# Three spaced groups of seven products in each FFN's down product, and x kept in two of five shared buffers

## The chip, the cores and the metric

The kernel runs on one core of one Trainium2 chip. The metric is the device time of one execution in microseconds. Three executions of the kernel before took 1870.79, 1872.24 and 1873.25 us; their median, 1872.24 us, is the time before. The core works with a tensor engine (PE, with its weight loads shown apart as PEld), a vector engine (DVE), a scalar engine (ACT), GpSimd (POOL), and a sync engine (SP) that issues most of the transfers.

## The reference

One layer of a streaming encoder on 256 rows of width 2048, all in float32:

```
x += 1/2 * (silu(n1 @ w_gate) * (n1 @ w_up)) @ w_down      n1 = RMSNorm(x)      (FFN 1)
u | q | k | v = RMSNorm(x) @ w_in
x += concat(RMSNorm(S5(u)), RMSNorm(attention(q, k, v))) @ w_out
x += 1/2 * (silu(n2 @ w_gate) * (n2 @ w_up)) @ w_down      n2 = RMSNorm(x)      (FFN 2)
x += RMSNorm((p @ w_ple_proj) * sigmoid(RMSNorm(x) @ w_ple_gate))
```

The hidden width of the FFNs is 5632. The two products `@ w_down` (256 x 5632 by 5632 x 2048) are what the change is about; w_gate and w_up are 2048 x 5632 each.

## The kernel before

**Precision.** Every float32 operand of a matmul is split into a rounded part and a rest (`split`, L165 to L173): a cast on ACT writes `hi` (L168), a subtraction on DVE writes `lo` (L171). A product is then three matmuls: hi by hi, lo by hi, hi by lo.

**Tiles.** The 256 rows are two row tiles `t` of 128. Weights come in raw tiles of 128 x 4 x 512 (four blocks of 128 along the contraction, one column block of 512; 1 MB, one transfer on SP, L282). A raw tile is split in two halves of 128 x 1024, `whi` and `wlo`, in four buffers each. A half feeds 12 matmuls of 128x128 by 128x512: two blocks, two row tiles, three matmuls (`gemm_half`, L285). Raw tiles have three buffers. So PE can be at most about four halves behind DVE, and the transfers at most three raw tiles ahead of the splits.

**FFN.** The hidden values are written as `hT` (transposed blocks of 32 that SP's small transfers set in order, L216). `act(k)` (L586) splits four of the 44 contraction blocks into `hhi` and `hlo`, in two buffers. The down product before goes through the four column blocks of 512 one after the other (L591): eleven raw tiles each, `act(k)` made anew for each of them, the sum of a column block in two banks of PSUM (tag `acc`, four of them), then two instructions that add half of it to the residual x (L594), then the next norm's work for this block (`nxt.block`, L357: DVE transposes, sixteen small transfers on SP, four scaled splits, squares on ACT).

**Groups of seven.** In FFN 2 the first four contraction blocks of gate and up are already done together, by seven products of sums in place of eight (`gemm_seven`, L428, Winograd's form of Strassen's scheme). The left-hand sums are made once (`sum_forms`, L409); the right-hand sums are four DVE additions of weight halves (L459), whose splits go to `shi` and `slo`, three buffers each. The order is products 1, 2, 5, 6, 4, 7, 3. The other twelve contraction blocks follow as plain columns. FFN 1 has no such groups.

**Order.** The program hands the instructions over in an order, and a planner orders them per engine from that. `step()` (L100) is called after each half and moves side work (`put_off`) on by one.

**x.** The residual x is in eight tiles of its own (pool `xres`, L53 and L140) from start to end. It is read for the squares of the first norm, changed by the down product of FFN 1, by w_out, by the down product of FFN 2, and by the last line.

Of the kernel before, what the change touches and what calls it, by code (L numbers as in the profile page):

```python
# [33 lines left out]
def layer_kernel(ctx: ExitStack, tc: tile.TileContext, a: dict, shapes: dict, out: bass.AP):  # L34
# [18 lines left out]
    xpool = ctx.enter_context(tc.tile_pool(name="xres", bufs=1))  # L53
# [10 lines left out]
    def uid(s):  # L64
        count[0] += 1
        return f"{s}_{count[0]}"
# [161 lines left out]
    def in_32(u):  # L228
        return u.rearrange("p j (x b) -> p j x b", b=32)
# [7 lines left out]
    def first_quarters(w, xn):  # L237

        rest = com("h")
        raws = [wp.tile([P, 4, NB], F32, tag="raw", name=uid("raw"), bufs=3) for _ in range(2)]  # L240
# [36 lines left out]

    def weight_halves(w, k0, nk, n0, own=None):

        raw = wp.tile([P, 4, NB], F32, tag="raw", name=uid("raw"), bufs=3)  # L280
        src = w[k0 * P : (k0 + nk) * P, n0 : n0 + NB].rearrange("(j p) n -> p j n", p=P)
        nc.sync.dma_start(raw[:, :nk, :], src)  # L282
        return weight_split(raw, nk, own)
# [122 lines left out]
        def rs(self, t):  # L406
            return self.r[:, t : t + 1]

    def sum_forms(parts):  # L409

        hi, lo = parts
        whole, sums = com("h"), com("h")
        u = whole.rearrange("p (j t m) -> p j t m", j=4, t=TT)
        nc.vector.tensor_tensor(
            out=whole.rearrange("p (j t) -> p j t", j=4), in0=hi.bitcast(F32), in1=lo.bitcast(F32), op=ALU.add
        )
        s = sums.rearrange("p (z j m) -> p z j m", z=4, j=2)
        up, down = u[:, :2], u[:, 2:]
        for z, (x, y, op) in enumerate((
            (up[:, :, 1], down[:, :, 1], ALU.subtract), (s[:, 0], up[:, :, 0], ALU.subtract),  # L420
            (up[:, :, 0], up[:, :, 1], ALU.subtract), (down[:, :, 0], s[:, 1], ALU.add),
        )):
            nc.vector.tensor_tensor(out=s[:, z], in0=x, in1=y, op=op)
        both = halves("n")
        split(*both, sums.rearrange("p (z t) -> p z t", z=4))
        return both

    def gemm_seven(act, sums, ws, n0, nkt, pool, first, second):  # L428

        raws = []  # L430
        for w in ws:
            raw = wp.tile([P, 4, NB], F32, tag="raw", name=uid("raw"), bufs=3)
            nc.sync.dma_start(raw, w[: 4 * P, n0 : n0 + NB].rearrange("(j p) n -> p j n", p=P))
            raws.append(raw)
        b11, b21, b12, b22 = (raw[:, 2 * h : 2 * h + 2, :] for raw in raws for h in range(2))
        parts = act(0)

        def whole(k, t):
            return [[u[:, 2 * k + j, t * P : (t + 1) * P] for j in range(2)] for u in parts]

        def summed(z):
            return [[u[:, z, j * P : (j + 1) * P] for j in range(2)] for u in sums]

        def product(ps, left, src, own, stop):
            hi, lo = (
                (pool if own else wp).tile([P, 2, NB], F32R, tag=s, name=uid(s), bufs=3 if own else None)
                for s in (("shi", "slo") if own else ("whi", "wlo"))
            )
            split(hi, lo, src)
            lh, ll = left  # L450
            for j in range(2):
                nc.tensor.matmul(ps, lhsT=lh[j], rhs=hi[:, j], start=j == 0, stop=False)  # L452
                nc.tensor.matmul(ps, lhsT=ll[j], rhs=hi[:, j], start=False, stop=False)  # L453
            for j in range(2):
                nc.tensor.matmul(ps, lhsT=lh[j], rhs=lo[:, j], start=False, stop=stop and j == 1)  # L455

        def add(x, y):
            t = pool.tile([P, 2, NB], F32, tag="sum", name=uid("sum"), bufs=2)
            nc.vector.tensor_tensor(out=t, in0=x, in1=y, op=ALU.add)  # L459
            return t  # L460

        p1, p2 = acc(), acc()
        product(p1, whole(0, 0), b11, False, True)
        product(p2, whole(1, 0), b21, False, False)
        step()
        t1 = add(b11, b12)
        p5 = acc()
        product(p5, summed(0), t1, True, True)
        t2 = add(t1, b22)
        p67 = aux()  # L470
        product(p67[:, :NB], summed(1), t2, True, True)
        step()
        t4 = add(t2, b21)
        p4 = acc()
        product(p4, whole(1, 1), t4, True, False)
        t3 = add(b12, b22)
        product(p67[:, NB:], summed(2), t3, True, True)
        step()
        p38 = aux()
        product(p38[:, :NB], summed(3), b22, False, False)  # L480
        step()
        put_off(0, first, p1, p67)
        for w, banks, fresh in ((ws[0], [p2, p4], False), (ws[1], [p38[:, :NB], p38[:, NB:]], True)):
            for k0 in range(4, nkt, 4):
                part = act(k0 // 4)
                for half in list(weight_halves(w, k0, 4, n0)):
                    begin = k0 == 4 and half[0] == 0
                    end = k0 + 4 >= nkt and half[0] == 1
                    for t in range(TT):
                        gemm_half({t: banks[t]}, (part, half), (t,), fresh and t == 1 and begin, end)  # L490
                    step()
            if not fresh:
                put_off(0, second, p2, p4, p5)
        return p38

    def ffn(i, xn, nxt, bg=None):
        wg, wu, wd = (a[f"ffn{i}_w_{s}"][0] for s in ("gate", "up", "down"))
# [22 lines left out]
        for f in range(NF):  # L520
# [5 lines left out]
            if sevens and f:  # L526
                sg, hh = com("sg"), com("h")
                gate_cols, up_cols = ([u[:, t * NB : (t + 1) * NB] for t in range(TT)] for u in (sg, hh))

                def opened(p1, p67, g=gate_cols, u=up_cols):  # L530
                    nc.scalar.copy(g[0], p1)
                    nc.vector.tensor_tensor(out=u[0], in0=p67[:, :NB], in1=g[0], op=ALU.add)
                    nc.vector.tensor_tensor(out=u[1], in0=p67[:, NB:], in1=u[0], op=ALU.add)

                def gated(p2, p4, p5, g=gate_cols, u=up_cols, hh=hh):
                    for z, (ps, other) in enumerate(((p2, g[0]), (p4, u[1]))):
# [3 lines left out]
                    nc.vector.tensor_tensor(  # L540
                        out=v, in0=p5.unsqueeze(1).to_broadcast([P, TT, NB]), in1=v, op=ALU.subtract
                    )

                p38 = gemm_seven(xn, sums, (wg, wu), f * NB, KD, sevens, opened, gated)
                nc.vector.tensor_tensor(out=hh, in0=p38, in1=hh, op=ALU.add)
# [15 lines left out]
            if f == 0 and not bg:  # L561
                both = gemm_pair(xn, ((wg, 0), (wu, 0)), KD)
                pg = next(both)
                sums = sum_forms(xn(0))
            else:
                pg = gemm_block(xn, wg, f * NB, KD, first)
            sg = com("sg")
# [15 lines left out]
                )  # L583
            put_off(2, turned, hp, f, hh)

        def act(k):  # L586
            hi, lo = halves("h")
            split(in_32(hi), in_32(lo), hT[k // 2][:, k % 2 * 4 : k % 2 * 4 + 4])
            return hi, lo

        for n in range(ND):  # L591
            ps = gemm_block(act, wd, n * NB, F // P)
            for t in range(TT):
                nc.vector.scalar_tensor_tensor(  # L594
                    out=xt[t][n], in0=ps[t], scalar=0.5, in1=xt[t][n], op0=ALU.mult, op1=ALU.add
                )
            put_off(0 if n == ND - 1 and n < nxt.early else 2, nxt.block, n)
        pools.close()


# [734 lines left out]
    for n, side in ((0, 0), (1, 0), (0, 1), (1, 1), (2, 0), (2, 1), (3, 0), (3, 1)):  # L1335
        y, r = ((yss, rss), (ysb, rsb))[side]
        ps = next(both) if n < 2 and not side else gemm_block(lambda k: y[k], sides[side], n * NB, SW // P)
        for t in range(TT):
            nc.vector.scalar_tensor_tensor(
                out=xt[t][n], in0=ps[t], scalar=r[0][:, t : t + 1], in1=xt[t][n], op0=ALU.mult, op1=ALU.add  # L1340
            )
        if side:
            put_off(0 if n == ND - 1 else 2, n2.block, n)
    atp.close()
    mix.close()
# [205 lines left out]
```

## Time and profile before

| | |
|---|---|
| median of three executions | 1872.24 us |
| the profiled execution | 1872.24 us |
| its span, first to last instruction | 1870.4 us |
| granted clock of the tensor engine | 1.000 |
| matmuls, busy share of PE | 9134, 99% |
| busy share of PEld, DVE, ACT, POOL | 82%, 70%, 53%, 3% |
| share of 16 DMA engines, transfers issued by SP | 63.7% |
| down product of FFN 1 | about 491 to 730 us |
| gate and up of FFN 2 with groups of seven | about 1097 to 1523 us |
| down product of FFN 2 | about 1523 to 1763 us |

The span is what lies between the first and the last instruction. A matmul record is longer than the distance to the next one, since matmuls are pipelined; what counts is the distance from start to start. In the lists, "idle before" is the time an engine stood still before an instruction, with what ended it. Idle time of ACT or DVE costs nothing as long as PE is fed.

### The profile page before, as it was taken

The numbers are of one execution on the slowest core, as the hardware profiler recorded it, in microseconds if no ns is written. First come the engines' busy times: TensorE is split into PE (matmuls) and PEld (weight loads), VectorE is DVE, ScalarE is ACT, GpSimd is POOL, SyncE is SP. The second block draws the span as 40 slices with busy tenths as digits, with TensorE's granted clock in tenths as the row PEclk, the third lists the DMA queues.
The fourth block names the chain that finished last, engine by engine and source line by source line (L and its number), as shares of the span: only waits on it lengthen the run. The fifth ranks groups of instructions, "written<-read, shape, count | busy, mean of one in ns | idle before, by whom it ended". The sixth has DMA issues, their size and how long they took to land.

```text
span 1870.4 us, 23938 instructions
## 1 busy us (share of the span) xinstructions
PE 1859.4 (99%) x9134; PEld 1536.3 (82%) x9134; DVE 1310.4 (70%) x1527; ACT 996.5 (53%) x1151; POOL 50.4 (3%) x84
## 2 busy tenths in 40 slices
PE   9999999999999999999999999999999999999998
PEld 7888888888888888878888888888888888888887
DVE  8867665455576776687567678778787866777655
ACT  7444444444456665456695555445454555666554
POOL 0011000000000000010020000000000000000000
PEclk9999999999999999999999999999999999999999
DMA  8788867766655666675645666575666675656563
GB/s 323 242 278 268 267 208 222 231 217 200 217 196 199 212 199 244 185 248 163 222 147 189 218 205 221 203 220 186 203 205 208 225 228 203 204 202 212 189 224 124
DMA packets 230387, 400.06 MB, mean 214 GB/s; under 512 B 26401, under 2 KB 50337, under 8 KB 229985
## 3 DMA queue, kind: packets, MB, share of 16 engines
q1 hardware_dynamic: 227824, 392.81, 63.7%
q0 software_dynamic: 1728, 4.33, 0.7%
q8 instruction: 71, 1.16, 0.3%
q10 hardware_dynamic: 720, 1.41, 0.2%
q14 instruction: 44, 0.35, 0.1%
HBM read 369.26 MB, written 9.83 MB: 203 GB/s over the span
## 4 chain that ended last, share of the span: by engine, by line
PE 92%; ACT 3%; DVE 2%; DMA 1%; SPq 1%; issue 1%; POOL 0%; DVEq 0%; ACTq 0%; POOLq 0%
PE acc L292 26%; PE acc L297 26%; PE acc L293 26%; PE aux L293 3%; PE aux L292 3%; PE aux L297 3%; ACT whi L168 1%; SPq L1061 1%; PE acc L455 1%; DMA raw<-in_w_in 1%; PE aux L452 1%; PE acc L452 1%; PE acc L453 1%; PE aux L455 1%; PE aux L453 1%
## 5 line engine op out<-in xcount | busy, mean ns | idle before, releaser
L171 DVE TENSOR_TENSOR wlo<-raw,whi 128x1024 fp32r<-128x1024 f32 x656 | 798.2, 1224 | 458.9 <-ACT whi L168 455.3
L168 ACT CAST whi<-raw 128x1024 fp32r<-128x1024 f32 x656 | 686.2, 1053 | 758.7 <-PE acc L293 607.9
L292 PE MATMUL acc<-whi,nhi 128*128 128x512 f32 x1408 | 551.0, 391 | 1.2 <-ACT whi L260 0.5
L293 PE MATMUL acc<-whi,nlo 128*128 128x512 f32 x1408 | 548.2, 389 | 0.0
L297 PE MATMUL acc<-wlo,nhi 128*128 128x512 f32 x1408 | 384.4, 389 | 0.0
L292 PE MATMUL acc<-whi,hhi 128*128 128x512 f32 x816 | 317.6, 389 | 0.0
L293 PE MATMUL acc<-whi,hlo 128*128 128x512 f32 x816 | 317.5, 389 | 0.0
L292 PEld LDWEIGHTS acc<-whi,nhi 128*128 128x128 f32 x1408 | 264.3, 188 | 58.3 <-ACT whi L168 1.7
L297 PEld LDWEIGHTS acc<-wlo,nhi 128*128 128x128 f32 x1408 | 264.2, 188 | 55.6 <-DVE wlo L171 0.4
L293 PEld LDWEIGHTS acc<-whi,nlo 128*128 128x128 f32 x1408 | 264.4, 188 | 54.0
L297 PE MATMUL acc<-wlo,hhi 128*128 128x512 f32 x816 | 221.0, 389 | 0.0
L297 PEld LDWEIGHTS acc<-wlo,hhi 128*128 128x128 f32 x816 | 152.8, 188 | 32.5 <-DVE wlo L171 0.9
L293 PEld LDWEIGHTS acc<-whi,hlo 128*128 128x128 f32 x816 | 153.2, 188 | 32.0
L292 PEld LDWEIGHTS acc<-whi,hhi 128*128 128x128 f32 x816 | 153.1, 188 | 31.8
L171 DVE TENSOR_TENSOR hlo<-hT,hhi 128x1024 fp32r<-128x1024 f32 x88 | 107.1, 1218 | 0.0
L168 ACT CAST hhi<-hT 128x1024 fp32r<-128x1024 f32 x88 | 91.8, 1044 | 0.5 <-PE acc L455 0.4
L292 PE MATMUL aux<-whi,nhi 128*128 128x512 f32 x160 | 62.2, 389 | 0.0
L293 PE MATMUL aux<-whi,nlo 128*128 128x512 f32 x160 | 62.2, 389 | 0.0
L297 PE MATMUL aux<-wlo,nhi 128*128 128x512 f32 x160 | 49.3, 389 | 0.0
L171 DVE TENSOR_TENSOR slo<-sum,shi 128x1024 fp32r<-128x1024 f32 x40 | 48.6, 1214 | 0.4 <-ACT shi L168 0.2
L168 ACT CAST shi<-sum 128x1024 fp32r<-128x1024 f32 x40 | 42.1, 1052 | 11.5 <-DVE sum L459 11.4
L297 PEld LDWEIGHTS aux<-wlo,nhi 128*128 128x128 f32 x160 | 30.0, 188 | 6.2
(312 smaller groups left out, 1314.5 us busy)
## 6 DMA issues: line engine op xcount, KB each, us to landing
raw<-in_ffn_w_up SPq DMA_DIRECT2D x88, 1024.0 KB, 5.9
raw<-in_ffn_w_down SPq DMA_DIRECT2D x88, 1024.0 KB, 5.0
raw<-in_ffn_w_gate SPq DMA_DIRECT2D x86, 1024.0 KB, 5.4
raw<-in_w_in SPq DMA_DIRECT2D x32, 1024.0 KB, 5.5
raw<-in_w_out SPq DMA_DIRECT2D x16, 1024.0 KB, 5.1
raw<-in_w_ple_gate SPq DMA_DIRECT2D x16, 1024.0 KB, 5.1
hT<-mid SPq DMA_DIRECT2D x160, 64.0 KB, 5.0
h<-mid SPq DMA_DIRECT2D x176, 32.0 KB, 3.4
```

The lines of the kernel that those rows point to most:

```text
L168: copy = nc.scalar.copy(hi, src)
L171: nc.vector.tensor_tensor(out=lo, in0=src, in1=hi.bitcast(F32), op=ALU.subtract)
L292: nc.tensor.matmul(ps[t], lhsT=lh, rhs=hi[:, j, cols], start=start and j == 0, stop=False)
L293: nc.tensor.matmul(ps[t], lhsT=ll, rhs=hi[:, j, cols], start=False, stop=False)
L297: nc.tensor.matmul(ps[t], lhsT=lh, rhs=lo[:, j, cols], start=False, stop=stop and j == 1)
L452: nc.tensor.matmul(ps, lhsT=lh[j], rhs=hi[:, j], start=j == 0, stop=False)
L453: nc.tensor.matmul(ps, lhsT=ll[j], rhs=hi[:, j], start=False, stop=False)
L455: nc.tensor.matmul(ps, lhsT=lh[j], rhs=lo[:, j], start=False, stop=stop and j == 1)
L1061: nc.sync.dma_start(zt[0][p1 : p1 + HC, z], sv[p0 : p0 + HC, r % 2 * 2 + r // 2])
```

## The change

Four things change.

1. The pool of x goes. x lies in two raw buffers (`place_x`), and raw tiles get five buffers. The buffers of x are given back between its uses: x is read again at the start of the down product of FFN 1 from the input, and at that of FFN 2 from a scratch tensor `scr_x`, which w_out's end writes. These transfers (8 of 256 KB for each, `fetch_x`, and 8 for the write) are issued on POOL.
2. The down product handles two column blocks at once, with all eight PSUM banks. A plain step `c` multiplies four contraction blocks into both column blocks, and splits `act` once for both (`kept`). A step `s` does the same four by a group of seven. `a5` does the rest, side by side. The first pair has two groups, the second one.
3. Since the left-hand sums differ from group to group, `sum_forms` runs for each, from `hT`; the results of the products that both columns share are added to x as soon as the last group of a pair is through (`opened`).
4. `gemm_seven` becomes a class, used in FFN 2's gate and up too, with its products in the order 1, 5, 6, 4, 7, 2, 3. A pool `sums1` is opened for FFN 1's down product.

```diff
-    xt = [[xpool.tile([P, NB], F32, name=f"x_{t}_{n}") for n in range(ND)] for t in range(TT)]
+    def place_x():
+        for t in range(TT):
+            x = wp.tile([P, ND, NB], F32, tag="raw", name=uid("x"), bufs=5)
+            xt[t][:] = [x[:, n, :] for n in range(ND)]
+
+    def fetch_x(rows):
+        place_x()
+        for n in range(ND):
+            for t in range(TT):
+                nc.gpsimd.dma_start(xt[t][n], rows[t * P : (t + 1) * P, n * NB : (n + 1) * NB])
...
-        raw = wp.tile([P, 4, NB], F32, tag="raw", name=uid("raw"), bufs=3)
+        raw = wp.tile([P, 4, NB], F32, tag="raw", name=uid("raw"), bufs=5)
...
+        def chunk(self, kb, final=()):
+            raws = []
+            for w, n0 in self.ws:
+                raw = wp.tile([P, 4, NB], F32, tag="raw", name=uid("raw"), bufs=5)
...
+                raws.append(raw)
+            b11, b21, b12, b22 = (raw[:, 2 * h : 2 * h + 2, :] for raw in raws for h in range(2))
+            parts, sums = self.act(kb), self.sums(kb)
...
+            self.product(1, whole(0, 0), b11, False, final)
+            t1 = self.add(b11, b12)
+            self.product(5, summed(0), t1, True, final)
+            step()
+            t2 = self.add(t1, b22)
+            self.product(6, summed(1), t2, True, final)
+            t4 = self.add(t2, b21)
+            self.product(4, whole(1, 1), t4, True, final)
+            step()
+            t3 = self.add(b12, b22)
+            self.product(7, summed(2), t3, True, final)
+            self.product(2, whole(1, 0), b21, False, final)
+            step()
+            self.product(3, summed(3), b22, False, final)
+            step()
+
+        def column(self, side, kbs, final=False):
+            zs = ((2, 4), (3, 8))[side]
+            w, n0 = self.ws[side]
+            for kb in kbs:
+                part = self.act(kb)
+                for half in list(weight_halves(w, 4 * kb, 4, n0)):
+                    end = final and kb == kbs[-1] and half[0] == 1
+                    for t in range(TT):
+                        ps = self.bank(zs[t])
+                        gemm_half({t: ps}, (part, half), (t,), self.begin(zs[t]), end)
+                    step()
...
-        for n in range(ND):
-            ps = gemm_block(act, wd, n * NB, F // P)
-            for t in range(TT):
-                nc.vector.scalar_tensor_tensor(
-                    out=xt[t][n], in0=ps[t], scalar=0.5, in1=xt[t][n], op0=ALU.mult, op1=ALU.add
-                )
-            put_off(0 if n == ND - 1 and n < nxt.early else 2, nxt.block, n)
+        def opened(s, n):
+            sg = com("sg")
+            one, six = sg[:, :NB], sg[:, NB:]
+            nc.scalar.copy(one, s.bank(1))
+            nc.vector.tensor_tensor(out=six, in0=s.bank(6), in1=one, op=ALU.add)
+            gather(xt[0][n], one, 0.5)
+            for t in range(TT):
+                gather(xt[t][n + 1], s.bank(5), 0.5)
+            gather(xt[0][n + 1], six, -0.5)
+            nc.vector.tensor_tensor(out=one, in0=s.bank(7), in1=six, op=ALU.add)
+            gather(xt[1][n], one, 0.5)
+            gather(xt[1][n + 1], one, -0.5)
+
+        plans = (
+            ("c2", "c3", "s0", "c4", "c5", "c6", "s1", "c7", "c8", "c9", "c10"),
+            ("c1", "c2", "s0", "c3", "c4", "a5"),
+        )
+        for n in range(0, ND, 2):
...
+            for u in plan:
+                kb, final = int(u[1:]), u == plan[-1]
+                if u[0] == "s":
+                    left -= 1
+                    s.chunk(kb, () if left else shared)
+                    if not left:
+                        put_off(0, opened, s, n)
+                    continue
+                for side in range(2):
+                    s.column(side, (kb,) if u[0] == "c" else range(kb, F // P // 4), final)
+                    if final:
+                        end(side)
```

Here `end(side)` adds a column block's two own banks to x (two instructions as at L594) and puts off `nxt.block` for it, and `gather` is the instruction of L594 with a scale.

More of the change, by code (lines that the diff above doesn't have):

```diff
@@ L239, in first_quarters @@
         rest = com("h")
[L240 removed]
+        raws = [wp.tile([P, 4, NB], F32, tag="raw", name=uid("raw"), bufs=5) for _ in range(2)]
         src = [w[i * NB : (i + 1) * NB, :NB].rearrange("(j p) n -> p j n", p=P) for i in range(2)]
@@ L457, in add @@
-        def add(x, y):
-            t = pool.tile([P, 2, NB], F32, tag="sum", name=uid("sum"), bufs=2)
+                nc.tensor.matmul(ps, lhsT=lh[j], rhs=lo[:, j], start=False, stop=z in final and j == 1)
+        def add(self, x, y):
+            t = self.pool.tile([P, 2, NB], F32, tag="sum", name=uid("sum"), bufs=2)
             nc.vector.tensor_tensor(out=t, in0=x, in1=y, op=ALU.add)
             return t
-        p1, p2 = acc(), acc()
-        product(p1, whole(0, 0), b11, False, True)
-        product(p2, whole(1, 0), b21, False, False)
@@ L491, in gemm_seven @@
                     step()
-            if not fresh:
-                put_off(0, second, p2, p4, p5)
-        return p38
+    shared = (1, 5, 6, 7)
     def ffn(i, xn, nxt, bg=None):
```

146 lines of the change are left out of this document (84 added, 62 removed).

## The prediction

> **What bounds the kernel now.** I read the page's busy times first, then the waits, then the stages one by one.
>
> ```profile
> span 1870.4 us, 23938 instructions
> PE 1859.4 (99%) x9134; PEld 1536.3 (82%) x9134; DVE 1310.4 (70%) x1527; ACT 996.5 (53%) x1151; POOL 50.4 (3%) x84
> ```
>
> PE is busy for 99% of the span, so all other engines have room on the average. The waits say who follows whom:
>
> ```profile
> ACT whi L168 <- PE acc L293: 607.9, 432, 3.0
> DVE wlo L171 <- ACT whi L168: 455.3, 385, 7.4
> ACT whi L168 <- DMA raw<-in_ffn_w_gate: 22.2, 10, 5.1
> ```
>
> ACT's cast of a weight half stood still 432 times until PE had let go of a `whi` buffer. So the splits run as far ahead of PE as four buffers allow, and wait there. The stage of FFN 2's down product, and PE's chain at its start:
>
> ```profile
> 1523.40:1763.00 239.60, 239.60 (x1059) 198.40 (x1058) 170.63 (x160) 142.41 (x156) 0.00 (x0) 1.00 0.61 208
> ```
> ```profile
> 1523.45 0.23 PE acc L292
> ...
> 1526.17 0.23 PE acc L292
> ```
>
> The columns of the first are the stretch, its length, then the busy time of PE, PEld, DVE, ACT and POOL, the granted clock 1.00, the share of the DMA engines and GB/s. PE never stops. From one half's first matmul to the next half's it is 2.72 us for 12 matmuls: 0.2267 us each. The stage has 4 column blocks x 22 halves x 12 = 1056 matmuls, 239.4 us at this rate, and took 239.6. So a matmul taken out here is worth 0.2267 us, as long as PE stays fed.
>
> **The matmuls removed.** A plain step on two column blocks has 4 halves x 12 = 48 matmuls, a group of seven 7 x 6 = 42. There are three groups in each FFN's down product, six in all: 36 matmuls, 36 x 0.2267 = 8.2 us less.
>
> The page's PEld row, 1536.3 us in 9134 loads, is 0.168 us each, well under 0.2267. The Trainium skill (Perfetto Trace Analysis, Identifying the Most-Contended Engine) holds matmul busy time to be a poor measure of headroom, and points to the share of weight loads instead, here 82%. If only that were worth something, the 36 would give 6.1 us rather than 8.2. The stage's own length, 0.2267 us per matmul with no pause, speaks against that, and the sum goes by it.
>
> **What a group asks of DVE.** The prices, from groups and timelines:
>
> ```profile
> 1181.33 1.23 DVE L171 TENSOR_TENSOR slo<-sum,shi 128x1024 fp32r<-128x1024 f32 x1
> 1182.47 1.22 DVE L171 TENSOR_TENSOR wlo<-raw,whi 128x1024 fp32r<-128x1024 f32 x1
> 1183.61 1.22 DVE L545 TENSOR_TENSOR h<-aux,h 128x1024 f32<-128x1024 f32 x1
> ```
> ```profile
> L423 DVE TENSOR_TENSOR h<-h,h 128x256 f32<-128x256 f32 x2 | 0.8, 422 | 0.0
> L594 DVE SCALAR_TENSOR_TENSOR x<-acc,x 128x512 f32<-128x512 f32 x16 | 10.3, 686 | 8.7 <-PE acc L297 8.7
> L180 DVE SCALAR_TENSOR_TENSOR nlo<-h,gains,nhi 128x256 fp32r<-128x256 f32 x52 | 22.8, 489 | 1.2 <-ACT nhi L178 1.2
> ```
>
> DVE starts its 1024-wide instructions 1.14 us apart. A plain step needs four `wlo` and one `hlo`, 5.7 us of DVE in 48 x 0.2267 = 10.9 us of PE. A group needs `hlo`, four left-hand sums of 0.42, `nlo`, seven `lo` splits and four additions: 13 x 1.14 + 1.7 = 16.5 us of DVE in 42 x 0.2267 = 9.5 us of PE. It draws 7.0 us on the lead. How large is the lead?
>
> ```profile
> 1514.92 1.05 ACT L168 CAST whi<-raw 128x1024 fp32r<-128x1024 f32 x1 [0.71 <-ACT hhi L168]
> 1516.01 1.23 DVE L171 TENSOR_TENSOR wlo<-raw,whi 128x1024 fp32r<-128x1024 f32 x1 [0.35 <-ACT whi L168]
> 1523.29 0.39 PE L292 MATMUL acc<-whi,hhi 128*128 128x512 f32 x1
> ```
>
> These are one half's cast, its split, and PE's first matmul on it. DVE is through at 1517.15, 6.1 us before PE begins that half, and 8.9 us before PE begins the next one. So call T the start of PE on a group: DVE begins on it at T - 8.9. In the program's order it ends `hlo` at -7.8, the sums at -6.1, `nlo` at -4.9, then product 1 at -3.8, 5 at -1.5, 6 at 0.8, 4 at 3.1, 7 at 5.3, 2 at 6.5, 3 at 7.6. PE takes 1.36 us per product and wants the `lo` part 0.9 us after a product begins: at 0.9, 2.3, 3.6, 5.0, 6.3, 7.7 and 9.1. The tightest is product 7 with 1.0 us to spare. A group that starts with a full lead is covered. Between the two groups of the first pair lie three plain steps, which give back 3 x (10.9 - 5.7) = 15.6 us, more than the 7.0 drawn. ACT has nine casts at the 1.05 us shown, 9.5 us, in the same time, and is no bound.
>
> **What stands behind the last group of a pair.** There `opened` adds the shared products to x, eight DVE instructions of 0.61 us (L594's pairs, 1.3 us for two), 4.9 us, after an ACT copy. Queued behind it on DVE are the splits of the second column. After the group: `hlo` 8.7, two `wlo` 9.9 and 11.0, `opened` 15.9, the next `wlo` 17.1, wanted at 9.5 + 5.4 + 0.9 = 15.9: up to 1.2 us late. In the second pair the norm's scaled splits for two column blocks come due in the same step, since both blocks of the first pair ended together: L180 four times each, 1.7 us for one block ahead of that split, so up to 2.9 us late. Worst case over both FFNs: 2 x 1.2 + 2 x 2.9 = 8.2 us; best case 0, and no gain below it, since PE can't run faster than fed. In between, the groups in gate and up show how PE behaves when DVE is this late:
>
> ```profile
> 1148.86 0.93 PE aux L455 x4
> ...
> 1489.84 0.97 PE aux L455 x4
> ```
>
> Between these lie eight of the ten blocks with a group, 42.62 us each. Each has 42 + 144 = 186 matmuls, 42.16 us. Only 0.46 us per block is lost, although DVE is busy without pause there. PE's order has other matmuls between. I take 0.2 us for a first group, 0.6 for the one with `opened`, and 1.0 for the one with `opened` and the norms: 1.8 per FFN, 3.6 us.
>
> The saved `act` splits (44 before, 28 after per FFN) and the rest of the added DVE work lie beside PE and cost nothing: DVE was busy 170.6 of 239.6 us. If DVE filled up, that cover would be gone at once.
>
> **Gate and up of FFN 2.** The ten groups lose 10 x 0.46 = 4.6 us now. The new order splits products 1 and 5 first. The old one put two `wlo` ahead of the first addition:
>
> ```profile
> 1177.66 1.23 DVE L171 TENSOR_TENSOR wlo<-raw,whi 128x1024 fp32r<-128x1024 f32 x1 [1.45 <-ACT whi L168]
> 1178.80 1.22 DVE L459 TENSOR_TENSOR sum<-raw,raw 128x1024 f32<-128x1024 f32 x1
> ```
>
> This `wlo` waited for a `whi` buffer and the addition stood behind it. In the new order the addition has one such wait fewer in front, 2.72 us, and five raw buffers bring its weights sooner. Product 7, the last with an addition, is wanted at the same place but product 2 is then later by one split, so up to 0.23 us per group could be lost instead: bounds -4.6 and +2.3. I take half the loss, -2.3 us.
>
> **x and the transfers.** What was the cost of load and store of x elsewhere:
>
> ```profile
> raw<-in_ffn_w_down SPq DMA_DIRECT2D x88, 1024.0 KB, 5.0
> h<-mid SPq DMA_DIRECT2D x176, 32.0 KB, 3.4
> x<-in_x SPq DMA_DIRECT2D x8, 256.0 KB, 8.6
> coef<-scr_coef POOLq DMA_DIRECT2D x32, 64.0 KB, 6.6
> L788 POOL DMA_DIRECT2D coef<-scr_coef x32 | 15.4, 489 | 64.3 <-DVE t L841 57.4 <-DMA scr_coef<-cft 4.8 <-DMA coef<-scr_coef 1.2
> ```
>
> POOL gets 24 transfers of 256 KB more, at some 0.5 us of issue each 12 us on an engine that is 3% busy. Nothing waits for x until `opened`, some 70 us into the first pair. Its 2 MB delay weight tiles a little; the lead of a tile covers it. Bounds 0 and, if one tile per FFN came late by the 3.6 us between 5.0 and 8.6, 7.2 us; I take 0. SP gets two norm blocks' small transfers at once, 32 of them in the second pair at the pace of this row:
>
> ```profile
> 1587.91 2.51 SPq L216 DMA_DIRECT2D h<-mid  x4
> ```
>
> 0.63 us each, 20 us, spread over plain steps and the group, with raw tiles issued between: nothing, since the norm's splits come 13 halves later.
>
> **The sum.** -8.2 (matmuls) + 3.6 (late DVE) - 2.3 (gate and up) = -6.9 us. The profiled execution took 1872.24 us with 1870.4 us of span, and is itself the median. 1872.2 - 6.9 = 1865.3 us.
>
> **Rivals.**
>
> All is covered. PE fills each gap with ready matmuls, the loss in gate and up goes too: 1872.2 - 8.2 - 4.6 = 1859.4 us. For it: the table above has room at each product. Against it: the same room did not quite do in gate and up.
>
> DVE behind the groups gives the gain back: the worst case of 8.2 us, gate and up unchanged, 1872.2 us, no difference. For it: the planner keeps to program order on DVE, as L459 behind `wlo` shows, and `opened` is eight instructions in a row.
>
> The raw buffers bind (slower). During a down product x holds two of five, three are left, and a group holds two until its last split. In the new order product 2's split is the last reader of the first tile, up to T + 6.5, instead of the fourth addition. The tile that follows is issued then, lands after L, is cast in 1.05 us, and is wanted at T + 9.5 + 5.4 = 14.9: it is late when L exceeds 14.9 - 6.5 - 0.4 - 1.05 = 7.0 us. The median is 5.0, but all raw tiles spread widely:
>
> ```profile
> DMA to landing us min/median/max: 3.2/5.4/10.8
> ```
>
> With two tiles issued together and 9 us each, six groups lose 2 us, 12 us beyond my sum: 1877.3 us; at 10.8 us, 3.8 x 6 = 22.8, 1888 us. Against it: gate and up had three buffers, and the waits there (22.2 us on ACT) hardly reached PE.
>
> **Chances.** The forecast 0.50, all covered 0.14, gain given back 0.20, raw buffers 0.16. Two runs of this kernel can be told apart at about 0.2%, 3.7 us. The forecast and the first rival are faster, the second is within, the third slower; a little of the forecast's spread falls within 3.7 us, which I set off against the second's: faster 0.63, same 0.21, slower 0.16. The range goes from all covered to the raw buffers at 9 us: 1859.4 to 1877.3 us.
>
> **What would show it.** In the profile after: 36 matmuls fewer; FFN 2's down product about 235.4 + 1.8 = 237.2 us long in place of 239.6; blocks of gate and up with a group at 42.4 us in place of 42.62; in the second pair, behind the group, PE waiting for DVE's `wlo`. Wrong it is if ACT's casts there wait for raw tiles and PE with them (third rival), if a group has PE idle by more than 2 us, or if x's tiles keep weight tiles from being issued at the start of a down product.

## The result, and the profile after

| | before | after |
|---|---|---|
| median of four executions each | 1872.32 us | 1860.15 us |
| lowest and highest | 1870.79, 1873.25 us | 1859.97, 1860.21 us |
| the profiled execution, and its span | 1872.24, 1870.4 us | 1859.97, 1858.1 us |

The ratio is 0.9934, with a 95% interval of 0.9921 to 0.9947: faster by 0.66%, some 12 us. The page after, and two lines of its waits (engine, what it waited for, total us, times, longest):

```profile
span 1858.1 us, 23916 instructions
...
PE 1848.8 (100%) x9098; PEld 1530.4 (82%) x9098; DVE 1350.9 (73%) x1599; ACT 991.8 (53%) x1147; POOL 62.8 (3%) x108
```
```profile
ACT whi L181 <- PE acc L306: 497.9, 336, 3.0
DVE wlo L184 <- ACT whi L181: 398.7, 319, 7.3
```

There are 36 matmuls fewer, 9134 to 9098. DVE's share rose from 70% to 73%, and ACT and DVE still mostly wait for PE to let go of weight buffers.

Where did the 12.3 us between the two profiled executions go? The same five places in both traces mark the stages: the last hidden block of FFN 1; the four matmuls that stand ahead of the norm's eight transposes behind FFN 1's down product; the one plain hidden block of FFN 2; its last hidden block with a group; and the first result of the last line. Before, four rows of the timeline (start, length, engine, line, operation) and one of the chain:

```profile
490.41 1.41 DVE L580 SCALAR_TENSOR_TENSOR h<-acc,sm,sg 128x512 f32<-128x512 f32 x2 [1.09 <-PE acc L297]
...
1098.72 1.40 DVE L580 SCALAR_TENSOR_TENSOR h<-acc,sm,sg 128x512 f32<-128x512 f32 x2
...
1523.49 1.23 DVE L545 TENSOR_TENSOR h<-aux,h 128x1024 f32<-128x1024 f32 x1 [0.86 <-PE aux L297]
...
1802.39 1.27 ACT L1375 ACTIVATE h<-acc,sm 128x512 f32<-128x512 f32 x2
```
```profile
737.21 0.91 PE acc L297 x4
```

and after:

```profile
490.49 1.41 DVE L628 SCALAR_TENSOR_TENSOR h<-acc,sm,sg 128x512 f32<-128x512 f32 x2 [1.09 <-PE acc L310]
...
1092.92 1.40 DVE L628 SCALAR_TENSOR_TENSOR h<-acc,sm,sg 128x512 f32<-128x512 f32 x2
...
1514.93 1.23 DVE L593 TENSOR_TENSOR h<-aux,h 128x1024 f32<-128x1024 f32 x1 [0.86 <-PE aux L310]
...
1790.11 1.27 ACT L1476 ACTIVATE h<-acc,sm 128x512 f32<-128x512 f32 x2
```
```profile
733.57 0.91 PE acc L310 x4
```

| stage | before | after | difference |
|---|---|---|---|
| down product of FFN 1 | 246.80 | 243.08 | -3.7 |
| the middle: w_in, S5, attention, w_out, the first block of gate and up | 361.51 | 359.35 | -2.2 |
| gate and up of FFN 2 with groups | 424.77 | 422.01 | -2.8 |
| down product of FFN 2 | 278.90 | 275.18 | -3.7 |
| start and end of the span | | | +0.1 |

The two pairs of FFN 2's down product, then gate and up of FFN 2 from the first block with a group to the last, as stretches with busy times (columns as in the prediction):

```profile
1514.90:1632.10 117.20, 117.20 (x517) 96.85 (x517) 95.23 (x95) 63.45 (x64) 0.00 (x0) 1.00 0.59 200
1632.10:1750.60 118.50, 118.50 (x524) 97.99 (x523) 92.95 (x96) 73.33 (x89) 0.00 (x0) 1.00 0.66 219
```
```profile
1134.40:1514.90 380.50, 380.50 (x1675) 314.19 (x1675) 304.73 (x297) 194.05 (x199) 4.36 (x8) 1.00 0.67 214
```

PE never stops in any of them, as it did not before in the down product. The first pair has 528 - 12 = 516 matmuls, 117.0 us at 0.2267 us, and took 117.2. (Lengths of pairs below are taken from the last hidden block's row, and from the rows that add a pair's last column block to x.) The rest lies in the groups themselves. This is the first matmul of FFN 1's second group, and the first one behind the group:

```profile
554.55 0.39 PE L480 MATMUL acc<-whi,hhi 128*128 128x512 f32 x1
...
564.19 0.39 PE L305 MATMUL acc<-whi,hhi 128*128 128x512 f32 x1
```

The 42 matmuls between took 9.64 us without a pause, 229.5 ns each in place of 226.7: 0.12 us more for the group. All 16 groups of this trace, in the down products and in gate and up, have this distance; no run shows why it is longer. In gate and up, before, PE stood still for a little:

```profile
1140.10:1523.50 383.40, 382.83 (x1675) 312.73 (x1674) 304.67 (x296) 191.54 (x199) 0.00 (x0) 1.00 0.66 213
```

The nine blocks between the first and the last end took 383.3 / 9 = 42.59 us each before, and 380.5 / 9 = 42.28 after, where 186 matmuls at 0.2267 us make 42.16; the 0.12 left after is the group's longer distance. The waits of this stage show what went. Before, weight tiles came late, and PE then waited for splits:

```profile
ACT whi L168 <- DMA raw<-in_ffn_w_gate: 15.2, 8, 2.4
...
PEld aux L452 <- ACT shi L168: 2.7, 5, 0.6
```

After, the same view of the same stage has no line of a raw tile and none in which PE or its weight loads wait.

### The profile page after: what moved, and what is told of

Same layout as the page of the kernel before. It is cut to its first block, busy times and chain, and to the rows that moved or that the text cites. A ratio compares the mean times of both kernels' runs of the same rounds, so it can differ in the third digit from the quotient of the medians.

```text
span 1858.1 us, 23916 instructions
## 1 busy us (share of the span) xinstructions
PE 1848.8 (100%) x9098; PEld 1530.4 (82%) x9098; DVE 1350.9 (73%) x1599; ACT 991.8 (53%) x1147; POOL 62.8 (3%) x108
## 4 chain that ended last, share of the span: by engine, by line
PE 96%; ACT 2%; DVE 1%; DMA 0%; POOL 0%; issue 0%; SPq 0%; DVEq 0%; POOLq 0%
PE acc L305 22%; PE acc L310 22%; PE acc L306 22%; PE aux L306 7%; PE aux L305 7%; PE aux L310 7%; PE acc L480 2%; PE acc L481 2%; PE acc L483 2%; PE aux L480 1%; PE aux L481 1%; PE aux L483 1%; PE aux L1114 0%; ACT whi L181 0%; DMA raw<-in_ffn_w_gate 0%; ACT nhi L191 0%
## 5 line engine op out<-in xcount | busy, mean ns | idle before, releaser
L305 PE MATMUL acc<-whi,hhi 128*128 128x512 f32 x416 | 161.8, 389 | 0.0
L306 PE MATMUL acc<-whi,hlo 128*128 128x512 f32 x416 | 161.8, 389 | 0.0
L305 PE MATMUL aux<-whi,hhi 128*128 128x512 f32 x384 | 149.4, 389 | 0.0
L306 PE MATMUL aux<-whi,hlo 128*128 128x512 f32 x384 | 149.4, 389 | 0.0
L310 PE MATMUL acc<-wlo,hhi 128*128 128x512 f32 x416 | 126.7, 389 | 0.0
L310 PE MATMUL aux<-wlo,hhi 128*128 128x512 f32 x384 | 118.2, 389 | 0.0
L306 PEld LDWEIGHTS acc<-whi,hlo 128*128 128x128 f32 x416 | 78.1, 188 | 16.2
L305 PEld LDWEIGHTS acc<-whi,hhi 128*128 128x128 f32 x416 | 78.1, 188 | 16.2
L310 PEld LDWEIGHTS acc<-wlo,hhi 128*128 128x128 f32 x416 | 78.1, 188 | 16.2
L310 PEld LDWEIGHTS aux<-wlo,hhi 128*128 128x128 f32 x384 | 72.1, 188 | 15.0
```

What stands on the lines that cost most here:

```text
L305: nc.tensor.matmul(ps[t], lhsT=lh, rhs=hi[:, j, cols], start=start and j == 0, stop=False)
L306: nc.tensor.matmul(ps[t], lhsT=ll, rhs=hi[:, j, cols], start=False, stop=False)
L310: nc.tensor.matmul(ps[t], lhsT=lh, rhs=lo[:, j, cols], start=False, stop=stop and j == 1)
```

## The experiments

All times are medians in us; the kernel before, run beside them on the same chips, took 1871.57 (first four), 1871.36 (next four) and 1870.85 (last three). The kernel after has only its first four executions, beside which the kernel before took 1872.32: differences to 1860.15 carry this shift of up to 1.5 us, and the stage lengths from the traces are the surer ones.

**No groups.** How much of the gain is the removed matmuls, and does x in the raw buffers cost anything by itself? Every step of the down products is plain:

```diff
-            ("c2", "c3", "s0", "c4", "c5", "c6", "s1", "c7", "c8", "c9", "c10"),
-            ("c1", "c2", "s0", "c3", "c4", "a5"),
+            ('c0', 'c1', 'c2', 'c3', 'c4', 'c5', 'c6', 'c7', 'c8', 'c9', 'c10'),
+            ('c0', 'c1', 'c2', 'c3', 'c4', 'a5'),
```

> The changed kernel with every group of seven in the two down products made a plain step: the pairs of column blocks, x in two of five buffers and the new order in gate and up stay. It has as many matmuls as the kernel before. If the groups bring what the two traces say (36 matmuls of 0.2267 us less about 0.7 us of stalls), it takes 1860.15 + 7.4 = 1867.6 us. If part of the gain comes from handling two column blocks at once (fewer splits), it is well under that: 1864 us. If gate and up's gain needs nothing of the groups, their ten blocks stay at 42.28 us each.

It took 1867.73 (ratio to before 0.9980, 0.9972 to 0.9989). The groups are worth 1867.73 - 1860.15 = 7.6 us, of 36 x 0.2267 = 8.2. The 0.6 us that are missing are those of the groups' longer distance, 6 x 0.12 = 0.7: their DVE work costs PE nothing that shows. The other 3.8 us of the gain are there without them, 2.8 of them in gate and up, whose nine blocks take 42.28 us like those after. Two column blocks at once and x fetched on POOL thus cost nothing that shows.

**The old order in gate and up.** The prediction put the gain there down to the order 1, 5, 6, 4, 7, 2, 3. Here gate and up alone go back to the old one, with five raw buffers:

```diff
+            if early_two:
+                self.product(1, whole(0, 0), b11, False, final)
+                self.product(2, whole(1, 0), b21, False, final)
+                step()
+                t1 = self.add(b11, b12)
+                self.product(5, summed(0), t1, True, final)
...
-                s.chunk(0, shared)
+                s.chunk(0, shared, True)
```

> The changed kernel, with gate and up's groups in the order of before (products 1, 2, 5, 6, 4, 7, 3); the down products keep the new order. Theory order: the 0.32 us per block that gate and up gained comes from the first addition standing behind one cast fewer; then 1863.1 us, blocks of 42.6 us. Theory buffers: it comes from five raw buffers; then 1860.15 us, blocks of 42.28 us.

**x stays.** The buffers of x are never given back, so that three are left for weights everywhere, as before; the order is the new one:

```diff
-        fetch_x(a["x"][0] if bg else scr_x)
...
-            for t in range(TT):
-                nc.gpsimd.dma_start(scr_x[t * P : (t + 1) * P, n * NB : (n + 1) * NB], xt[t][n])
```

> The changed kernel, with x put into its two raw buffers once and left there: no second and third reading, no scratch tensor, and three raw buffers for weights everywhere, as before. Theory order: 1860.15 us, blocks of gate and up 42.28 us. Theory buffers: 1863.1 us, blocks of 42.6 us. If reading x again costs anything, it is gone here as well and the time falls below 1860 us.

**The kernel before with the new order** (and its three raw buffers):

```diff
-        p1, p2 = acc(), acc()
+        p1 = acc()
         product(p1, whole(0, 0), b11, False, True)
-        product(p2, whole(1, 0), b21, False, False)
-        step()
         t1 = add(b11, b12)
...
         product(p67[:, NB:], summed(2), t3, True, True)
+        p2 = acc()
+        product(p2, whole(1, 0), b21, False, False)
         step()
```

> The kernel before, with only the order of the products in gate and up's groups changed to 1, 5, 6, 4, 7, 2, 3. Theory order: 1872.3 - 3.0 = 1869.3 us. Theory buffers: 1872.3 us. Its instructions up to 1097 us are those of before, so the pause of 1.45 us in the tensor engine at 821 us, which the changed kernel doesn't have, should be there if it hangs on where the instructions lie.

The three give, with the kernels before and after, a table of block times in gate and up (span of the nine blocks, by nine) beside the medians:

| | order 1, 2, 5, 6, 4, 7, 3 | order 1, 5, 6, 4, 7, 2, 3 |
|---|---|---|
| three raw buffers | 42.59 (before) | 43.56 (before with new order, 1878.91, ratio 1.0037, 1.0025 to 1.0050) |
| three left beside x | | 43.21 (x stays, 1871.71, ratio 0.9999, 0.9990 to 1.0008) |
| five raw buffers | 42.28 (old order, 1860.03, ratio 0.9940, 0.9928 to 0.9953) | 42.28 (after, 1860.15) |

The order does nothing with five buffers, and with three the new one costs 0.6 to 1.0 us a block. No expectation had foreseen this: they put the kernel before with the new order at 1869.3 or 1872.3 us, and x staying at 1860.2 or 1863.1. The buffers make the gain, and keep the new order from costing what it costs with three, 7.3 us by the medians (1878.91 - 1871.57). Why, the place of a block's first addition `t1` shows, against the end of the block before it (the row `h<-aux,h`). Before, then after, then with x staying:

```profile
1178.80 1.22 DVE L459 TENSOR_TENSOR sum<-raw,raw 128x1024 f32<-128x1024 f32 x1
1183.61 1.22 DVE L545 TENSOR_TENSOR h<-aux,h 128x1024 f32<-128x1024 f32 x1
```
```profile
1164.91 1.22 DVE L487 TENSOR_TENSOR sum<-raw,raw 128x1024 f32<-128x1024 f32 x1
...
1177.53 1.22 DVE L593 TENSOR_TENSOR h<-aux,h 128x1024 f32<-128x1024 f32 x1
```
```profile
1172.73 1.22 DVE L486 TENSOR_TENSOR sum<-raw,raw 128x1024 f32<-128x1024 f32 x1
...
1176.58 1.22 DVE L592 TENSOR_TENSOR h<-aux,h 128x1024 f32<-128x1024 f32 x1
```

With five buffers the group's DVE work begins 12.6 us before the other block ends, with three 4.8 us (old order) or 3.9 us (new order). An addition reads both raw tiles of its group: both must be there while the tiles of the columns before are still held. With x staying, ACT waits in this stage for the tiles once more:

```profile
ACT whi L180 <- DMA raw<-in_ffn_w_gate: 29.4, 13, 2.9
```

The executions with x staying lay from 1868.14 to 1873.42; the profiled one is the lowest, 8.2 us above that after, and its nine blocks account for (43.21 - 42.28) x 9 = 8.4 us of it. In four of them PE stands still for 1.5 us, until ACT has split a sum. The kernel before with the new order has the same four pauses, and right behind two of them, at 1361.4 and at 1450.1 us, the granted clock (before the DMA share in the row) was halved for 3.4 us:

```profile
1360.98 0.50 PE L452 MATMUL acc<-shi,hhi 128*128 128x512 f32 x1 [1.47 <-ACT shi L168]
```
```profile
1361.40:1364.80 3.40, 3.40 (x10) 2.63 (x9) 3.40 (x5) 1.05 (x1) 0.00 (x0) 0.51 0.99 339
```

These two blocks took 45.96 and 45.95 us, the other two 44.39 and 44.35. Without the 1.6 us that a half clock cost each, this kernel too is at 43.21 us a block. The higher executions with x staying have no profile, but their mean clocks fall as their times rise: 1.000 at 1868.14 and 1868.25, 0.999 at 1869.67 and 1869.79, 0.998 or 0.997 from 1871.53 on, 0.997 at 1873.26 and 1873.42. One such stretch takes 0.0009 off the mean clock, so up to three of them, 4.8 us by an estimate from the blocks above, would nearly account for the spread of 5.3 us. No trace of those executions shows it.

**Two groups next to each other.** The prediction's lead, made up in plain steps between groups, is tested by leaving the steps out:

```diff
-            ("c2", "c3", "s0", "c4", "c5", "c6", "s1", "c7", "c8", "c9", "c10"),
+            ('c2', 'c3', 's0', 's1', 'c4', 'c5', 'c6', 'c7', 'c8', 'c9', 'c10'),
```

> The changed kernel, with the first pair's two groups one right after the other (c2 c3 s0 s1 c4 ... in place of c2 c3 s0 c4 c5 c6 s1 c7 ...), in both FFNs; the number of matmuls is the same. Theory lead: a group draws DVE's lead of 8.9 us down by 12 x 1.14 - 9.5 = 4.2 us when its left-hand sums are done earlier, and nothing gives it back before the second, whose sums (2.8 us) fall into the first; the two want 11 us of 8.9, of which 1 to 2 must remain: 2 to 4 us lost in each FFN, 1864 to 1868 us. Theory that the tensor engine's order fills every gap: 1860.2 us.

It took 1867.05 (0.9976, 0.9966 to 0.9987), 6.9 us above the kernel after: 3.3 us in the first pair of each FFN, and the second pairs alike. The chain of waits there runs over DVE, from about 502 to 541 us; these are three links of it one after the other (start, length):

```profile
524.36 1.14 DVE slo L184
525.50 1.13 DVE sum L487
526.63 1.14 DVE wlo L184
```

The lead is real: two groups in a row use it up, and PE loses 6.9 of the 7.6 us that the groups had brought.

**The left-hand sums bound to the group.** After, the sums read `hT`, which is there from the start, so that they can be made at any time. Here they read the group's own `hhi` and `hlo`, as gate and up do:

```diff
-            s = Seven(kept, lambda kb: sum_forms(sevens, rows(kb)), ((wd, n * NB), (wd, (n + 1) * NB)), sevens)
+            s = Seven(kept, lambda kb: sum_forms(sevens, whole_rows(sevens, kept(kb))), ((wd, n * NB), (wd, (n + 1) * NB)), sevens)
```

> The changed kernel, with the left-hand sums of the six groups made from the split activations (one DVE addition of 1.14 us more), so that they can't be done before the group's own act split. This is the work that the prediction put into the group, and 1.14 us on top: 17.7 us of DVE against 9.5. If the prediction's loss (3.6 us) was avoided because the sums were done some 20 us ahead, it comes back, with up to 1.1 us more per group: 1863 to 1870 us. If the groups would have had room anyway: 1860.2 to 1861 us.

It took 1868.87 (0.9985, 0.9976 to 0.9995), 8.7 us above the kernel after: 0.9 us in a first pair and 3.3 and 3.7 in the second pairs. It also makes `hhi` + `hlo` again, one DVE instruction more per group. In FFN 1's second pair there is something else in it, in SP's queue and in the chain:

```profile
616.63 12.59 SPq L229 DMA_DIRECT2D h<-mid  x19
629.31 0.53 SPq L295 DMA_DIRECT2D raw<-in_ffn_w_down  x1
```
```profile
629.31 5.61 DMA raw<-in_ffn_w_down
```

A raw tile stood behind 19 small transfers of the norm, 12.6 us, and landed on the chain that PE's next work hung on. FFN 2's second pair has the same, with 19 transfers from 1644.90 us on. The kernel after has the same queue at the same place, the tile issued behind it at 628.44, and there its late tile delays nobody:

```profile
615.66 12.69 SPq L229 DMA_DIRECT2D h<-mid  x19
```

The first pairs, with two groups each, don't have these 19 transfers, and lost 0.9 us. In each second pair PE waited for the `wlo` that stands behind `opened`,

```profile
PE aux L310 <- DVE wlo L184: 1.7, 1, 1.7
```

and the chain runs over the late tile before that. So this run has two causes in it, and how the 3.3 and 3.7 us divide between DVE's lead and that queue was not told apart.

**Four raw buffers.** Does the third rival hold where buffers are fewer? x holds two, and two are left:

```diff
-            x = wp.tile([P, ND, NB], F32, tag="raw", name=uid("x"), bufs=5)
+            x = wp.tile([P, ND, NB], F32, tag="raw", name=uid("x"), bufs=4)
...
-                raw = wp.tile([P, 4, NB], F32, tag="raw", name=uid("raw"), bufs=5)
+                raw = wp.tile([P, 4, NB], F32, tag="raw", name=uid("raw"), bufs=4)
```

> The changed kernel with four raw buffers in place of five: while x is held, two are left for weights, and a group holds both until its last splits. Theory of the third rival (the buffers would bind one step further down): no tile can be on its way during a group, the next arrives some 5.5 us after the last split and its casts come 2 to 5 us late; 12 to 30 us over six groups, plus what four buffers cost gate and up (0 to 10 us): 1872 to 1900 us. If the raw buffers have nothing to do with it: 1860.2 us.

It took 1879.14 (1.0039, 1.0024 to 1.0054), 19.0 us above the kernel after. The down product of FFN 1, by its waits:

```profile
ACT whi L181 <- DMA raw<-in_ffn_w_down: 37.3, 19, 4.2
```

ACT waits there for raw tiles and PE behind it, as the rival says, but the four pairs lose only 6.0 us together, 1 us a group. The greater part, 11.5 us, is lost between the down product of FFN 1 and w_out, where x holds two buffers too and only two bring w_in: first the kernel after, then this one, from about the end of the down product to w_out's first result.

```profile
726.00:977.40 251.40, 249.50 (x1815) 210.62 (x1814) 171.84 (x209) 160.01 (x202) 19.22 (x22) 1.00 0.60 199
```
```profile
726.00:992.30 266.30, 256.14 (x1830) 214.44 (x1829) 174.05 (x212) 160.20 (x203) 18.29 (x22) 0.99 0.60 193
```

The second stretch holds 3.3 us of the down product as well, and 3.4 us at half clock behind a pause of PE (from 830.3 us on), which the 0.99 shows. In gate and up, where x is out of the way, four buffers do nearly as five (42.33 us a block). So it is five because of x.

**More groups.** If DVE has room, more groups should pay. Ten, eight, ten set wider, and ten with four of them in each first pair:

```diff
# ten: three groups in the first pair, two in the second
+            ('c2', 'c3', 's0', 'c4', 'c5', 's1', 'c6', 'c7', 's8', 'c9', 'c10'),
+            ('c1', 'c2', 's0', 'c3', 's4', 'a5'),
# eight: the first line of ten, and the second pair as after
+            ('c1', 'c2', 's0', 'c3', 'c4', 'a5'),
# ten, wider: the first line of ten, and
+            ('c1', 's0', 'c2', 'c3', 's4', 'a5'),
# four in the first pair, and the second pair as after
+            ('c2', 's0', 'c3', 'c4', 's1', 'c5', 'c6', 's7', 'c8', 's9', 'c10'),
```

> The changed kernel with three groups in the first pair (c2 c3 s0 c4 c5 s1 c6 c7 s8 c9 c10) and two in the second (c1 c2 s0 c3 s4 a5): ten groups in both FFNs in place of six, 24 matmuls fewer. Theory lead, with two plain steps giving back 10.4 us for 4.2 + 2.8 drawn: 1860.15 - 24 x 0.2267 = 1854.7 us; the second pair's two groups have one plain step between them and the norms, 1 to 3 us of loss in each FFN: 1855 to 1861 us. If it is 1860 or above, three groups is where DVE's room ends.

> The changed kernel with a third group in the first pair only (c2 c3 s0 c4 c5 s1 c6 c7 s8 c9 c10) and the second pair as it is. With ten groups the first pair was 1.2 us shorter in each FFN than with two, and the second pair 2.3 to 2.6 us longer. Theory lead: 1860.15 - 2 x 1.2 = 1857.7 us. If the third group's cost shows up somewhere later, 1860 us or more.

> Ten groups again, with the second pair's two further apart: c1 s0 c2 c3 s4 a5 in place of c1 c2 s0 c3 s4 a5. Theory lead: the first group has only one plain step behind the pair's start, where DVE has the last pair's sums and the norm's transposes to do (5 us), but the second has 10.4 us to recover and the norm's splits fall between the groups: 0.5 to 1.5 us of loss in each FFN for 1.36 us of gain, 1857 to 1860 us. If the second pair's loss hangs on the number of groups and not on their distance: 1863 us.

> The changed kernel with four groups in the first pair (c2 s0 c3 c4 s1 c5 c6 s7 c8 s9 c10), the second as it is. Two of them have one plain step between. Theory lead: one plain step gives back 5.2 us of the 7.0 us that a group draws, so the shortfall, 1.8 us, is still within the lead after two: 1855 to 1857 us. If one plain step between is too little, as it was in the second pair, 1858 to 1862 us.

| | median | ratio to before | first pairs (FFN 1, FFN 2) | second pairs |
|---|---|---|---|---|
| after (2 + 1 groups) | 1860.15 | 0.9934 (0.9921 to 0.9947) | 117.42, 117.20 | 118.44, 118.44 |
| ten (3 + 2) | 1862.99 | 0.9953 (0.9939 to 0.9968) | 116.19, 115.96 | 120.69, 121.02 |
| eight (3 + 1) | 1858.31 | 0.9933 (0.9920 to 0.9945) | 116.18, 115.96 | 118.46, 118.46 |
| ten, wider (3 + 2) | 1856.92 | 0.9924 (0.9911 to 0.9936) | 116.18, 115.96 | 117.83, 117.82 |
| four in the first (4 + 1) | 1858.36 | 0.9932 (0.9919 to 0.9946) | 115.66, 115.52 | 119.18, 119.21 |

A third group in the first pair, two plain steps from the next, gives 1.2 of its 1.36 us (6 x 0.2267). A second one in the second pair costs 2.3 to 2.6 us with one plain step between the two, and gives 0.6 with two (the first group stands one step earlier there as well). A fourth in the first pair gives 0.5, and the second pair behind it loses 0.7. The prediction's own prices fit this: a group draws 7.0 us on the lead, its left-hand sums with it wherever they are made; one plain step gives back 5.2, two give 10.4, less what `opened` and the norms take of it. The first ten groups, expected at 1855 to 1861 us, missed that by the places of the groups and not by their number. The page of the fastest of them, ten groups set wider, which beats both kernels (3.7 us less span than after, and its four pairs are 3.7 us shorter):

```profile
span 1854.4 us, 23932 instructions
...
PE 1845.0 (99%) x9074; PEld 1526.8 (82%) x9074; DVE 1388.7 (75%) x1647; ACT 1005.9 (54%) x1163; POOL 62.7 (3%) x108
```

60 matmuls fewer than before, 13.6 us at 0.2267.

## Why the prediction was right, and where it was not

The forecast was 1865.3 us, and 1860.15 lies inside the range, but nearer to "all is covered" (1859.4) than to the forecast. In part that is luck: the 2.2 us of the middle are not the change's, as is shown below, and without them the prediction's count would end near 1862. By its terms:

| term | predicted | measured |
|---|---|---|
| 36 matmuls at 0.2267 us | -8.2 | -8.2 |
| late DVE behind the groups | +3.6 | 0 |
| longer distance of the groups' matmuls | not thought of | +0.7 |
| gate and up of FFN 2 | -2.3 | -2.8 |
| x and the transfers | 0 | 0 |
| the middle (one execution of the kernel before, see below) | not thought of | -2.2 |
| start and end of the span | not thought of | +0.1 |
| sum | -6.9 | -12.4 (-12.3 by the profiled executions) |

**The matmuls.** Right: the two down products lost 7.4 us in the traces and 7.6 against the run without groups, 8.2 less the 0.7 by which the groups' other matmuls lie further apart. The prediction set beside this the Trainium skill (Perfetto Trace Analysis, Identifying the Most-Contended Engine), which judges TensorE's headroom by the share of weight loads, and by MFU. From that share, 82% here, the prediction made an estimate of 6.1 us. The measured 7.6 us does not bear the estimate out: with loads at 82%, a matmul out of PE's queue was worth 0.21 us of its 0.2267.

**Late DVE.** The term was 3.6 us, and in the trace after PE waits for nothing in the groups or behind them: FFN 2's down product took 235.6 us (1514.93 to 1750.57), where the prediction's sign was 237.2. The step that failed is "in the program's order it ends `hlo` at -7.8, the sums at -6.1, `nlo` at -4.9": the left-hand sums were put inside the group. In the trace after, PE begins FFN 1's second group at 554.55; on DVE its sums and `nlo` stand 28 to 34 us ahead of that, among plain steps where DVE waits for buffers anyway:

```profile
520.40 0.75 DVE L441 TENSOR_TENSOR rows<-hT 128x256 f32<-128x256 f32 x2
...
526.65 1.22 DVE L184 TENSOR_TENSOR nlo<-rows,nhi 128x1024 fp32r<-128x1024 f32 x1
...
530.95 1.22 DVE L184 TENSOR_TENSOR wlo<-raw,whi 128x1024 fp32r<-128x1024 f32 x1 [1.48 <-ACT whi L181]
...
546.78 1.22 DVE L487 TENSOR_TENSOR sum<-raw,raw 128x1024 f32<-128x1024 f32 x1
...
562.68 0.68 DVE L654 TENSOR_TENSOR sg<-aux,sg 128x512 f32<-128x512 f32 x1
...
566.28 1.22 DVE L184 TENSOR_TENSOR wlo<-raw,whi 128x1024 fp32r<-128x1024 f32 x1
567.41 1.29 DVE L648 SCALAR_TENSOR_TENSOR x<-sg,x 128x512 f32<-128x512 f32 x2
```

The group's first addition starts where the prediction has `hlo` end, at T - 7.8, and `opened` begins at T + 8.1 in place of T + 11.0. Nor does `opened` hold the queue for all of its eight instructions: a `wlo` goes ahead of its last two, through at T + 12.9 where the prediction had T + 17.1, and 15.9 would have been in time. The change gave the planner this freedom by taking the sums from `hT`; taking it away brought 8.7 us back, though how much of that is SP's queue was not told apart. The second rival, DVE that gives the gain back, is thus real, and shows nearly in full with two groups next to each other, but the spacing of the change keeps clear of it.

**Gate and up.** Right in size, wrong in its reason. "In the new order the addition has one such wait fewer in front" is what failed: with five buffers the old order takes the same time, and with three the new one is slower by 0.6 us a block, or 1.0 with the half clock. What the prediction named second, "five raw buffers bring its weights sooner", was all of it.

**The raw buffers bind.** Not in the kernel after: three left beside x are enough for a down product with groups. The mechanism was put rightly, and was found with three buffers in gate and up and with two left in the down product, at about 1 us a group, half of the 2 us that the prediction priced for three.

**x and the transfers.** Right, for the reason given: POOL's transfers, here those of FFN 2, take 0.55 us each, begin some 30 us before the down product, and find POOL idle: 434.4 us until a transfer of `hT` let the first one go, and 3.8 until DVE had read a raw tile. Nothing waits for them.

```profile
L150 POOL DMA_DIRECT2D x<-scr_x x8 | 4.4, 550 | 438.2 <-DMA hT<-mid 434.4 <-DVE wlo L184 3.8
```

"Spread over plain steps and the group, with raw tiles issued between" was too kind to SP's small transfers: 19 of them stand in a row. It cost nothing after, and did with the sums bound to the group.

**The middle.** The 2.2 us there were not foreseen, and the change did not bring them. The kernel before with the new order has, up to gate and up of FFN 2, the same instructions as the kernel before. From the row that adds FFN 1's last column block to x, to the first one of w_out, first before, then before with the new order:

```profile
729.77 1.29 DVE L594 SCALAR_TENSOR_TENSOR x<-acc,x 128x512 f32<-128x512 f32 x2 [1.09 <-PE acc L297]
...
983.02 1.40 DVE L1339 SCALAR_TENSOR_TENSOR x<-acc,sm,x 128x512 f32<-128x512 f32 x2
```
```profile
730.07 1.29 DVE L595 SCALAR_TENSOR_TENSOR x<-acc,x 128x512 f32<-128x512 f32 x2 [1.09 <-PE acc L297]
...
981.09 1.40 DVE L1340 SCALAR_TENSOR_TENSOR x<-acc,sm,x 128x512 f32<-128x512 f32 x2
```

That is 253.25 us and 251.02, and the kernel after took 251.09 (726.35 to 977.44). So the profiled execution of the kernel before was slow there by itself. Most of it is one pause of PE among 64 small matmuls, in the chain before:

```profile
820.50 0.95 PE aux L959 x51
821.46 1.45 issue
822.90 0.45 PE aux L959 x13
```

The trace names no wait for it. It does not stand at this place in any other trace here. Of the 12.3 us between the two profiled executions, then, 10.1 are the change's. How often the kernel before has such a pause is open; its executions spread over 2.5 us in the four shown, those after over 0.24.

## What to carry to other kernels

A stretch that differs where the change does nothing wants a second trace of the same instructions before it counts as gain: here 2.2 of 12.3 us were one execution's. Work that an engine does for a group need not be done at the group: ask what its inputs are and how early they are there, before putting it into a table of due times. Buffers that a long-lived tensor gives back between its uses can be worth more than the arithmetic saved (here the new order and the groups gained nothing by the medians with three raw buffers: 1871.71 against 1871.57 us). Where one engine must run ahead of another, count what each step draws on the lead and gives back; here two groups in a pair wanted two plain steps between them.

## What the runs showed of the hardware

Small transfers issued in a row on SP took 12.69 / 19 = 0.67 us each, and a weight tile behind them in the queue was issued only when they were through. DVE's 1024-wide instructions, shown with 1.22 us, followed each other at 1.14 us for a whole group without a pause (14 of them from 546.78 to 562.68). The matmuls of a group of seven lay 229.5 ns apart and those of plain steps 226.7, in every group of the trace after. Behind pauses of PE of 1.5 us, in the kernel before with the new order, the granted clock was halved for 3.4 us in two of four cases, matmuls then started 0.43 us apart, and each time cost 1.6 us; with x staying, the profiled execution had the same four pauses and no such stretch. And PE stood still for 1.45 us in one execution with nothing in the trace that it waited for, where another execution of the same instructions did not.
